# A two layer trunk kernel: the first weights issued from ScalarE's queue, and the half empty weight units stored densely

## The chip, the cores and the metric

The kernel runs on one core of one Trainium2 chip. The metric is device time in microseconds (us) of one execution. A core has five engines that run side by side and meet through semaphores: TensorE (PE, matrix products; its weight loads are listed as PEld), VectorE (DVE), ScalarE (ACT), GpSimd (POOL) and SyncE (SP), which here does nothing but issue DMAs. DMAs move data between HBM and the on-chip memory SBUF; SP, ACT and POOL can each issue them, every one into a queue of its own.

## What is computed

The reference is a trunk of two layers on 512 tokens of width 1024, in float32. Each layer is a mixer and a feed-forward block, each followed by a residual and a layer norm:

```
h = x
for layer in (0, 1):
    mix = even_mixer(h) if layer == 0 else odd_mixer(h)
    h = layer_norm(ALPHA * h + mix)
    h = layer_norm(ALPHA * h + conv_ffn(h))

even_mixer: x @ w_in -> conv + silu -> gated delta rule (6 heads), with beta = sigmoid(b), g from a
            x @ w_in -> dilated attention (3 groups, 4 heads);  concat @ w_out
odd_mixer:  x @ w_in -> differential attention (4 heads)
            x @ w_in -> gated linear attention (4 heads), its gate from g_d;  concat @ w_out
```

What matters here is the first product. The even mixer's narrow columns `b_a` and `a_a` (6 and 6) and the key columns of head 0 are needed for all 512 tokens before anything else can begin. The odd mixer has such a narrow piece too: the 16 columns `g_d`.

## The kernel before

All weights lie in one tensor `wts` of 128 x 1024 float32 units (512 KB each). A unit is eight blocks of 128 x 128, one for each 128 rows of the contraction (`k` = 0 to 7). The units 0 (`U_AB`: the columns of `b_a` and `a_a`) and `U_GG` (the columns `g_d`) are called NARROW: of each block only 64 columns hold anything, the other 64 are zeros.

Float32 products are made of float32r parts. A tile `x` of tokens becomes `xh` (a rounding CAST on ACT, line 252) and `xl = x - xh` (DVE, line 253). A weight unit becomes `wh` (ACT, line 493) and `wl` (DVE, line 494). A full unit costs three matmuls for each `k` (`mm3`, lines 481 to 483). A narrow unit keeps its high and low parts side by side in one tile, 64 columns each, and costs two (`narrow`, lines 501, 502 and 504).

`setup` (from line 205) starts everything. The tuple `START` gives the order in which the eight token tiles `("x", a, a + 1)` (256 KB each, 2 KB to a partition) and pieces of the first two units `(i, a, e)` (blocks `a` to `e` of unit `i`) are loaded. A first loop over `START` issues the loads, all of them on SP's queue (lines 223 and 226): 14 DMAs. Eight matmuls on a constant tile follow (`warm`, line 234). A second loop over `START` emits the CAST and the subtraction of each piece in the same order. Then `ask` asks for the units 2 and 3, whose loads (line 340) stand behind those of `START` on SP's queue, and the tables `par` and `con` follow (lines 261 and 262). Raw units pass through three buffers `wr`; units 0 and 1 hold two of them, so unit 2 takes the third and unit 3 waits until the last piece of unit 0 has been split.

`even` then emits the first products, `narrow` of step `k` ahead of `mm3` of step `k - 1`:

```
for k in range(KD + 1):
    if k < KD:
        self.narrow(pa, wa, k, self.xh[:, k, :], self.xl[:, k, :])
    if k:
        self.mm3(pb, wb, k - 1, ...)
```

After them come the tiles of the next units (`tile_of`, matmuls at line 366), with chains of other work in between, which a planner places by costs of its own. The chain `gates` takes the narrow product `pa` first; it begins with the load of an activation table (line 408). Instructions emitted through the planner all show line 159.

The order of instructions on an engine is the framework's: it lets an instruction forward when its simulated inputs are there earlier. `tc.keep_in_program_order` pins an instruction behind the one that was emitted before it on the same engine.

`U_GG` is loaded much later, by `unit` (line 474) inside the layer norm that ends layer 0, ahead of the odd mixer's first products in `lead`.

Of the kernel before, what the change touches and what calls it, by code (L numbers as in the profile page):

```python
# [9 lines left out]
F32 = mybir.dt.float32  # L10
# [7 lines left out]
P = 128  # L18
# [3 lines left out]
KD = D // P  # L22
# [36 lines left out]
for _n, _w in (("ident", 128), ("maskT", 128), ("nm1", 32), ("i32", 32), ("lm", 4 * 32), ("scan", 512),  # L59
# [30 lines left out]
EVEN_SEQ = "h0 h1 h2 h3 h4 h5 q00 v0 q01 v1 q02 v2 q10 q11 q12 z0 z1 z2 z3 z4 z5"  # L90
ODD_SEQ = "0D12G3abcd"

START = (("x", 0, 1), (0, 0, 2), ("x", 1, 2), (1, 0, 2), (0, 2, 5), ("x", 2, 3), ("x", 3, 4), (1, 2, 5), ("x", 4, 5),
         (0, 5, 8), ("x", 5, 6), ("x", 6, 7), (1, 5, 8), ("x", 7, 8))
WARM = 8
LEAD = 3
AHEAD = 2
# [97 lines left out]
class Trunk:  # L195
# [14 lines left out]
    def setup(self):  # L210
# [7 lines left out]
        self.xh = keep.tile([P, KD, S], F32R, name="xh")  # L218
        self.xl = keep.tile([P, KD, S], F32R, name="xl")
        first = [(u, self.wtiles()) for u in (U_AB, U_AB + 1)]  # L220
        for what, a, e in START:
            if what == "x":
                nc.sync.dma_start(self.h[:, a, :], self.xt[:, a, :])
            else:
                u, w = first[what]
                nc.sync.dma_start(w[0][:, a * P : e * P], self.wts[u][:, a * P : e * P])
        self.par = keep.tile([P, _NP], F32, name="par")
        self.con = keep.tile([P, _NCC], F32, name="con")
        self.ones = keep.tile([P, P], F32, name="ones")
        nc.gpsimd.memset(self.ones, 1.0 / P)  # L230

        warm = self.sps("warm")
        for _ in range(WARM):
# [233 lines left out]
    def unit(self, u, pool=None):  # L467
        nc = self.nc
        if u in self.asked:
            self.until(lambda: u in self.pre)  # L470
        if u in self.pre:
            return self.pre.pop(u)
        raw, wh, wl = self.wtiles(pool)
        nc.sync.dma_start(raw, self.wts[u])
        self.split(u, raw, wh, wl, nc.scalar, nc.vector)
        return wh, wl

# [7 lines left out]
    def split(self, u, raw, wh, wl, A, V, w=slice(0, KD * P)):  # L485

        if u in NARROW:
            raw, lo = (x[:, w].rearrange("p (k n) -> p k n", n=P) for x in (raw, wh))
            hi = lo[:, :, 0:64]
            raw, lo = raw[:, :, 0:64], lo[:, :, 64:P]  # L490
        else:
            raw, hi, lo = raw[:, w], wh[:, w], wl[:, w]
        A.copy(out=hi, in_=raw)  # L493
        V.tensor_tensor(out=lo, in0=raw, in1=hi.bitcast(F32), op=ALU.subtract)  # L494
# [1395 lines left out]
def _units(a):  # L1890
    def cols(w, off, n=P):

        x = w[:, off : off + n]
        if n < P:
            x = np.concatenate([x, np.zeros((w.shape[0], P - n), np.float32)], 1)
        return x

    def tile8(x, order=range(8)):
        b = x.reshape(8, P, P)
        return np.concatenate([b[k] for k in order], 1)  # L1900

    we, wo = a["w_in_even"][0], a["w_in_odd"][0]
    us = []

    def by_token(x):

        b, n = x.reshape(KD, P, x.shape[1]), 1024 // x.shape[1]
        for k in range(0, KD, n):
            us.append(np.concatenate(list(b[k : k + n]), 1))

    gq, gk, gv, gz, gb, ga = 0, 768, 1536, 2304, 3072, 3078
    ab = np.zeros((D, P), np.float32)
    ab[:, 0:6] = we[:, gb : gb + 6]
    ab[:, 32:38] = we[:, ga : ga + 6]
    us.append(tile8(ab))
    for h in range(6):
        for off in (gk, gq, gv):
            us.append(tile8(cols(we, off + h * P)))
    s0 = 3084
    for pair in range(2):  # L1920
        for g in range(3):
            for kind in range(2):
                us.append(tile8(cols(we, s0 + kind * 768 + g * 256 + pair * P)))
    for g in range(3):
        x = s0 + 2 * 768 + g * 256
        if g == 0:
            by_token(we[:, x : x + 256])
        else:
            for pair in range(2):
                us.append(tile8(cols(we, x + pair * P)))  # L1930
    for h in range(6):
        us.append(tile8(cols(we, gz + h * P)))
    for ft in range(8):
        us.append(tile8(cols(a["w_out_even"][0], ft * P), EVEN_ORDER))

    def ffn(l):
        up, dn = a["ffn_w_up"][l], a["ffn_w_down"][l]
        for f in range(NF):
            us.append(tile8(cols(up, f * P)))
            us.append(tile8(cols(up, DFF + f * P)))  # L1940
        b = dn.reshape(NF, P, 8, P).transpose(2, 0, 1, 3).reshape(22, 8, P, P)
        for u in range(22):
            us.append(np.concatenate(list(b[u]), 1))

    ffn(0)
    us.append(tile8(cols(wo, 3072, 16)))
    for pr in range(2):
        us.append(tile8(cols(wo, 1536 + pr * P)))
        us.append(tile8(cols(wo, 1792 + pr * P)))
    by_token(wo[:, 2048:2560])  # L1950
    by_token(wo[:, 1024:1536])
    for h in range(4):
        for off in (0, 512):
            us.append(tile8(cols(wo, off + h * P)))
    for h in range(4):
        us.append(tile8(cols(wo, 2560 + h * P)))
    for ft in range(8):
        us.append(tile8(cols(a["w_out_odd"][0], ft * P), ODD_ORDER))
    ffn(1)
    return np.ascontiguousarray(np.stack(us))  # L1960
# [31 lines left out]
```

## Time and profile before

| what | us |
|---|---|
| median of 3 runs | 1426.18 |
| lowest and highest of them | 1426.1, 1427.62 |
| the profiled execution's own time | 1425.01 |
| its span, first to last instruction | 1423.2 |
| TensorE busy in it | 1401.0 (98%) |

The profiled execution has 1.81 us outside its span, and it is 1.17 us below the median of the runs. A product of 512 columns takes PE 0.23 us from one start to the next, so the first products, 40 of them, are worth some 9.3 us of work.

In the rows below, a row of the order in time reads: start, duration, engine, line, operation, tiles, shape, how many, and in brackets how long the engine had been idle and what ended that. SPq and ACTq are DMA issues, whose duration is that of the issue and not of the transfer.

### The profile page before, as it was taken

How to read it: one execution, taken by the hardware profiler on the slowest of the kernel's cores; microseconds unless marked ns; L12 is line 12 of the kernel's file. 1: busy time of each engine (PE TensorE's matmuls, PEld its weight loads, DVE VectorE, ACT ScalarE, POOL GpSimd, SP SyncE). 2: the span in 40 equal slices, each digit the busy share in tenths (PEclk: the TensorE clock that was granted, in tenths of full speed). 3: DMA queues.
4: the chain of work that ended last, by engine and by line, in shares of the span. 5: the costliest groups of instructions: out<-in, count | busy, mean ns of one | idle time of the engine just before them, and what ended most of it. 6: DMA issues, size and time to landing. Idle time of an engine off the chain costs nothing.

```text
span 1423.2 us, 22725 instructions
## 1 busy us (share of the span) xinstructions
PE 1401.0 (98%) x9050; PEld 1146.4 (81%) x9050; DVE 840.7 (59%) x1636; ACT 673.9 (47%) x1285; POOL 177.6 (12%) x237
## 2 busy tenths in 40 slices
PE   8999999999999999999999999999999999999997
PEld 6878887777798888888888877878898888888886
DVE  6875755543696555555243797777776555553354
ACT  6644433744856444434131856557574444442233
POOL 2103012011023111111010310000131111110010
PEclk9999999999999999999999999999999999999998
DMA  7444112112232232232223313211313223223221
GB/s 248 151 130 125 61 50 72 55 61 65 90 119 90 89 97 95 90 99 94 96 97 104 92 55 105 74 46 60 119 38 120 95 90 100 93 89 104 89 74 59
DMA packets 41601, 130.94 MB, mean 92 GB/s; under 512 B 4653, under 2 KB 9629, under 8 KB 41496
## 3 DMA queue, kind: packets, MB, share of 16 engines
q1 hardware_dynamic: 36448, 120.36, 26.2%
q10 hardware_dynamic: 3464, 4.14, 1.1%
q0 software_dynamic: 1584, 5.00, 1.1%
q8 instruction: 71, 1.16, 0.3%
q14 instruction: 34, 0.28, 0.1%
HBM read 127.29 MB, written 5.29 MB: 93 GB/s over the span
## 4 chain that ended last, share of the span: by engine, by line
PE 84%; DVE 6%; ACT 5%; DMA 2%; issue 2%; POOL 1%; SPq 0%; ACTq 0%; DVEq 0%; POOLq 0%
PE pd L481 18%; PE pd L482 18%; PE pd L483 18%; PE pd L366 17%; PE pd L392 3%; PE pc L159 1%; PE po L159 1%; PE sps L159 1%; PE pz L159 1%; PE py L159 1%; DMA wr<-wts 1%; PE dsc L159 1%; PE pa L159 1%; PE dpo L159 1%; DVE s L553 1%
## 5 line engine op out<-in xcount | busy, mean ns | idle before, releaser
L494 DVE TENSOR_TENSOR wl<-wr,wh 128x1024 fp32r<-128x1024 f32 (+1 forms) x153 | 188.0, 1230 | 314.1 <-ACT wh L493 310.5
L481 PE MATMUL pd<-xh,wh 128*128 128x512 f32 (+1 forms) x968 | 356.4, 369 | 1.3 <-ACT wh L493 0.8
L482 PE MATMUL pd<-xl,wh 128*128 128x512 f32 (+1 forms) x968 | 357.0, 369 | 0.3 <-DVE xl L678 0.2
L483 PE MATMUL pd<-xh,wl 128*128 128x512 f32 (+1 forms) x968 | 356.3, 368 | 0.0
L493 ACT CAST wh<-wr 128x1024 fp32r<-128x1024 f32 (+2 forms) x157 | 160.0, 1025 | 208.5 <-PE pd L482 184.4
L482 PEld LDWEIGHTS pd<-xl,wh 128*128 128x128 f32 x968 | 181.6, 188 | 35.4 <-DVE xl L678 0.9
L481 PEld LDWEIGHTS pd<-xh,wh 128*128 128x128 f32 x968 | 181.3, 188 | 35.7 <-ACT wh L493 1.2
L483 PEld LDWEIGHTS pd<-xh,wl 128*128 128x128 f32 x968 | 181.6, 188 | 34.6 <-issue 0.8
L366 PE MATMUL pd<-xh,wh 128*128 128x512 f32 x424 | 173.0, 408 | 0.0
L366 PE MATMUL pd<-xl,wh 128*128 128x512 f32 x424 | 171.4, 404 | 0.0
L481 PE MATMUL pd<-ah,wh 128*128 128x512 f32 (+1 forms) x396 | 145.1, 366 | 0.0
L483 PE MATMUL pd<-ah,wl 128*128 128x512 f32 (+1 forms) x396 | 144.7, 365 | 0.0
L482 PE MATMUL pd<-al,wh 128*128 128x512 f32 (+1 forms) x396 | 144.7, 365 | 0.0
L715 DVE SCALAR_TENSOR_TENSOR y<-pd,par,y 128x510 f32<-128x510 f32 (+1 forms) x176 | 130.6, 747 | 2.8
L366 PE MATMUL pd<-xh,wl 128*128 128x512 f32 x424 | 118.8, 404 | 0.0
L724 POOL TENSOR_TENSOR al<-y,ah 128x512 fp32r<-128x512 f32 x44 | 59.1, 1343 | 419.8 <-ACT ah L723 419.8
L159 DVE TENSOR_TENSOR wl<-wr,wh 128x1024 fp32r<-128x1024 f32 x63 | 77.1, 1226 | 37.6 <-PE pd L366 14.7
L159 ACT CAST wh<-wr 128x1024 fp32r<-128x1024 f32 x63 | 65.8, 1047 | 61.4 <-PE pd L366 44.4
L366 PEld LDWEIGHTS pd<-xl,wh 128*128 128x128 f32 x424 | 79.8, 188 | 17.3 <-issue 1.9
L366 PEld LDWEIGHTS pd<-xh,wh 128*128 128x128 f32 x424 | 79.7, 188 | 16.9 <-issue 0.3
L366 PEld LDWEIGHTS pd<-xh,wl 128*128 128x128 f32 x424 | 76.4, 188 | 15.7 <-issue 0.7
L482 PEld LDWEIGHTS pd<-al,wh 128*128 128x128 f32 x396 | 74.7, 189 | 12.2
(386 smaller groups left out, 1866.9 us busy)
## 6 DMA issues: line engine op xcount, KB each, us to landing
wr<-wts SPq DMA_DIRECT2D x214, 512.0 KB, 3.4
h<-xt SPq DMA_DIRECT2D x16, 256.0 KB, 3.7
rep<-tab POOLq DMA_DIRECT2D x1, 3072.0 KB, 17.2
h<-gd POOLq DMA_DIRECT2D x6, 256.0 KB, 6.3
qe<-ge ACTq DMA_DIRECT2D x5, 256.0 KB, 6.1
bd<-rep ACTq DMA_DIRECT2D x1, 1024.0 KB
out<-h SPq DMA_DIRECT2D x2, 512.0 KB, 3.0
wr<-wts SPq DMA_DIRECT2D x4, 192.0 KB, 5.7
```

The lines of the kernel that those rows point to most:

```text
L159: r = fn(*a, **k)
L366: self.nc.tensor.matmul(ps, lhsT=w[part][:, k * P : (k + 1) * P], rhs=x[:, k, :], start=(i == 0), stop=(i == 23))
L392: self.nc.tensor.matmul(pss[b][:, a : a + n], lhsT=chunk(x[:, k, :], c), rhs=ws, start=(k == 0 and a == 0 and not part and x is self.xh), ...
L481: nc.tensor.matmul(ps, lhsT=wh, rhs=ah, start=first, stop=False)
L482: nc.tensor.matmul(ps, lhsT=wh, rhs=al, start=False, stop=False)
L483: nc.tensor.matmul(ps, lhsT=wl, rhs=ah, start=False, stop=last)
L493: A.copy(out=hi, in_=raw)
L494: V.tensor_tensor(out=lo, in0=raw, in1=hi.bitcast(F32), op=ALU.subtract)
L553: V.tensor_tensor(out=s2[:, a:e], in0=(self.q0 if ft == 1 else s2)[:, a:e], in1=q[:, : e - a], op=ALU.add)
L715: V.scalar_tensor_tensor(out=y[:, sft:], in0=ps[:, : S - sft], scalar=w(2 - sft), in1=y[:, sft:], op0=ALU.mult, op1=ALU.add)
L724: G.tensor_tensor(out=al[:, f, :], in0=y, in1=ah[:, f, :].bitcast(F32), op=ALU.subtract)
```

## The change

The loads of the first two units move from SP's queue to ACT's; the token tiles stay on SP's. On ACT they are pinned, in `START`'s order, behind a copy of one column (`idle`), which needs the constant tile `ones`; that tile's memset is emitted earlier for it. `START` itself is rewritten: unit 0 is loaded in two pieces and not three, so that there are 13 DMAs, eight on SP and five on ACT. The two narrow units are stored densely: eight blocks of 64 columns, then 512 columns of zeros. Their loads (in `setup` and in `unit`) take the first half only, 256 KB, and `split` reads the raw tile densely. The split parts, the products and everything after them stay.

```diff
-START = (("x", 0, 1), (0, 0, 2), ("x", 1, 2), (1, 0, 2), (0, 2, 5), ("x", 2, 3), ("x", 3, 4), (1, 2, 5), ("x", 4, 5),
-         (0, 5, 8), ("x", 5, 6), ("x", 6, 7), (1, 5, 8), ("x", 7, 8))
+START = (("x", 0, 1), (0, 0, 4), ("x", 1, 2), (1, 0, 2), ("x", 2, 3), (1, 2, 5), ("x", 3, 4), (0, 4, 8), ("x", 4, 5),
+         ("x", 5, 6), (1, 5, 8), ("x", 6, 7), ("x", 7, 8))
...
         first = [(u, self.wtiles()) for u in (U_AB, U_AB + 1)]
+
+        self.ones = keep.tile([P, P], F32, name="ones")
+        nc.gpsimd.memset(self.ones, 1.0 / P)
+        idle = keep.tile([P, 1], F32, name="idle")
+        tc.keep_in_program_order(nc.scalar.copy(out=idle, in_=self.ones[:, 0:1]))
         for what, a, e in START:
             if what == "x":
                 nc.sync.dma_start(self.h[:, a, :], self.xt[:, a, :])
             else:
+
                 u, w = first[what]
-                nc.sync.dma_start(w[0][:, a * P : e * P], self.wts[u][:, a * P : e * P])
+                n = 64 if u in NARROW else P
+                tc.keep_in_program_order(nc.scalar.dma_start(w[0][:, a * n : e * n], self.wts[u][:, a * n : e * n]))
         self.par = keep.tile([P, _NP], F32, name="par")
         self.con = keep.tile([P, _NCC], F32, name="con")
-        self.ones = keep.tile([P, P], F32, name="ones")
-        nc.gpsimd.memset(self.ones, 1.0 / P)
...
         raw, wh, wl = self.wtiles(pool)
-        nc.sync.dma_start(raw, self.wts[u])
+        n = KD * (64 if u in NARROW else P)
+        nc.sync.dma_start(raw[:, :n], self.wts[u][:, :n])
         self.split(u, raw, wh, wl, nc.scalar, nc.vector)
...
         if u in NARROW:
-            raw, lo = (x[:, w].rearrange("p (k n) -> p k n", n=P) for x in (raw, wh))
-            hi = lo[:, :, 0:64]
-            raw, lo = raw[:, :, 0:64], lo[:, :, 64:P]
+            lo = wh[:, w].rearrange("p (k n) -> p k n", n=P)
+            raw = raw[:, w.start // 2 : w.stop // 2].rearrange("p (k n) -> p k n", n=64)
+            hi, lo = lo[:, :, 0:64], lo[:, :, 64:P]
...
+    def narrow(x):
+
+        b = x.reshape(8, P, P)[:, :, :64]
+        return np.concatenate(list(b) + [np.zeros((P, 512), np.float32)], 1)
+
...
-    us.append(tile8(ab))
+    us.append(narrow(ab))
...
-    us.append(tile8(cols(wo, 3072, 16)))
+    us.append(narrow(cols(wo, 3072, 16)))
```

## Rows read from the trace of the kernel before

**Rows 1.** Busy time by stretch: length, engines (instructions), TensorE's clock, DMA share, GB/s.

```profile
0.00:5.20 5.20, 3.79 (x17) 3.50 (x17) 1.68 (x4) 2.10 (x3) 4.42 (x16) 1.00 0.53 151
5.20:18.10 12.90, 10.94 (x41) 6.98 (x41) 7.46 (x14) 9.28 (x17) 0.00 (x0) 1.00 0.99 335
18.10:1423.20 1405.10, 1386.29 (x8995) 1135.88 (x8993) 831.57 (x1619) 662.52 (x1267) 173.17 (x221) 1.00 0.28 90
```

**Rows 2.** The order in time on PE, 1 to 18.4 us.

```profile
1.01 3.79 PE L234 MATMUL warm<-ones 128*128 128x128 f32 x16 [1.01 <-POOL ones L230]
5.20 0.58 PE L501 MATMUL pd<-xh,wh 128*128 128x512 f32 x1 [0.40 <-DVE wh L494]
5.61 0.39 PE L502 MATMUL pd<-xl,wh 128*64 128x512 f32 x1
...
8.03 0.50 PE L481 MATMUL pd<-xh,wh 128*128 128x512 f32 x1 [0.84 <-ACT wh L493]
...
10.31 0.44 PE L502 MATMUL pd<-xl,wh 128*64 128x512 f32 x1 [0.23 <-DVE xl L253]
...
12.91 0.45 PE L502 MATMUL pd<-xl,wh 128*64 128x512 f32 x1
...
16.46 0.39 PE L502 MATMUL pd<-xl,wh 128*64 128x512 f32 x1
...
18.10 0.39 PE L366 MATMUL pd<-xh,wh 128*128 128x512 f32 x1
```

**Rows 3.** The order in time on ACT, 0 to 35 us.

```profile
0.75 1.28 ACT L252 ACT_TABLE_LOAD   x1 [0.75 <-PEq L1984]
3.60 0.62 ACT L252 CAST xh<-h 128x512 fp32r<-128x512 f32 x1 [1.56 <-DMA h<-xt]
...
7.57 0.40 ACT L493 CAST wh<-wr 128x256 fp32r<-128x256 f32 x1 [1.61 <-DMA wr<-wts]
...
8.92 0.62 ACT L252 CAST xh<-h 128x512 fp32r<-128x512 f32 x1 [0.42 <-DMA h<-xt]
9.44 0.19 ACT L159 CAST rp<-rb 33x4 fp32r<-33x4 f32 x1
...
14.52 0.62 ACT L252 CAST xh<-h 128x512 fp32r<-128x512 f32 x1 [0.16 <-DMA h<-xt]
15.16 1.28 ACT L408 ACT_TABLE_LOAD   x1
16.45 1.05 ACT L159 CAST wh<-wr 128x1024 fp32r<-128x1024 f32 x1
...
34.07 1.05 ACT L159 CAST wh<-wr 128x1024 fp32r<-128x1024 f32 x1 [0.94 <-PE pd L366]
34.08 0.84 ACTq L1128 DMA_DIRECT2D qe<-ge  x2
```

**Rows 4.** Busy time by stretch again, while the first loads run.

```profile
4.00:7.00 3.00, 2.36 (x8) 1.14 (x7) 1.59 (x3) 1.03 (x3) 0.96 (x2) 1.00 0.66 177
7.00:14.00 7.00, 5.28 (x20) 3.17 (x19) 4.37 (x10) 4.77 (x11) 0.00 (x0) 1.00 1.08 364
```

**Rows 5.** SP: its second issue, then what its queue waited for (us, times, longest).

```profile
1.19 0.42 SPq L226 DMA_DIRECT2D wr<-wts  x1
...
SPq L223 <- DMA wr<-wts: 1.0, 1, 1.0
```

**Rows 6.** The order in time on DVE: the subtraction of a piece of 128x256.

```profile
8.01 0.43 DVE L494 TENSOR_TENSOR wl<-wr,wh 128x256 fp32r<-128x256 f32 x1 [1.32 <-ACT wh L493]
```

**Rows 7.** Groups of 780 to 808 us, the odd mixer's narrow products: busy, mean ns, idle.

```profile
L501 PE MATMUL pd<-xh,wh 128*128 128x256 f32 x14 | 3.9, 278 | 0.0
```

**Rows 8.** Waits of PE over the whole span, the longest (us, times, longest).

```profile
PE pvt L159 <- ACT vf L159: 1.7, 1, 1.7
```

**Rows 9.** The trace's end: PE's last matmuls, then a stretch as in rows 1.

```profile
1412.42 0.59 PE L617 MATMUL sd<-sq,onesL 128*128 128x256 f32 x2
...
1415.00:1416.00 1.00, 0.00 (x0) 0.00 (x0) 1.00 (x5) 0.72 (x2) 0.50 (x1) 0.54 0.00 0
```

## The prediction

> **What bounds the kernel now.** I read busy time by stretch first. From 18.10 us to the end TensorE is busy 1386.29 of 1405.10 us [rows 1]: it sets the time, its work does not change here, and only 18.8 us in all are not matmul, the tail after its last product among them. So the change can act only by letting TensorE start that run earlier, and every microsecond gained before 18.10 is kept unless something else is late next.
>
> Before 18.10 the order in time on PE shows what is to be won. The seven starts from 16.46 to 18.10 give 0.234 us for one matmul; 40 of them are 9.4 us, and they take from 5.20 to 18.10, 12.9 us [rows 2]. So 3.5 us are lost. The reader is to see where: the subtraction of the first weights ends the wait at 5.20, the first piece of unit 1 that at 8.03 (0.84 us), and the low part of token tile 2 that at 10.31. From there to 12.91 stand ten steps, 2.34 us of work in 2.60, so tile 4 costs only 0.26 more; from 12.91 on there is no gap: 22 steps, 5.15 us, to 18.10. All of these are waits for DMAs behind ACT and DVE: ACT's CASTs of tile 0, of the piece at 7.57, of tile 2 and of tile 7 each begin when their transfer lands [rows 3].
>
> Busy time by stretch shows how the transfers run. From 7 to 14 us they move 364 GB/s with the DMA engines full (1.08); from 4 to 7 us it is 177 GB/s at a share of 0.66 [rows 4]. SP's queue at times waits for an earlier landing before it issues again (1.0 us once) [rows 5].
>
> **The change, part by part.**
>
> *Fewer bytes.* START falls from 3072 to 2816 KB (8 x 256 and 512 + 512, then 256 + 512). At 364 KB per us the whole group lands 0.7 us earlier, tile 7 with it, at some 13.8 and not 14.5 [rows 3, 4]. But tile 7 is not what TensorE waits for: after 12.91 it has no gap [rows 2]. What counts is how much is moved before tile 2, and then before tile 4. In the old order 1216 KB are moved up to the end of tile 2 (three tiles, pieces of 128, 128 and 192 KB) and 1920 up to that of tile 4. Now the weights come on a queue of their own, so the order is no longer given. If they come just as START lists them, it is 1024 and 1856 KB: 0.53 and 0.18 us earlier. If the two queues take turns packet by packet from the start, tile 2 ends with three pieces of weights as before (1216 KB, 0), and tile 4 with all five (2048 KB, 0.35 us later). The trace of before has no stretch with both queues full, so I keep both ends and take 0: the old order is almost in the middle.
>
> By the Trainium skill (DMA: Bandwidth & Descriptors, Queues, rings and completion order) each DMA engine goes round between the queues that have work, a packet at a time; by it the second end holds, and the sum would be 0.35 us later through tile 4. No run here shows it yet.
>
> *Two queues in the slow stretch.* From 4 to 7 us the engines moved 3 x (364 - 177) = 561 KB less than at the later rate, 1.54 us of transfer [rows 4]. This is before tile 2 lands at 8.92, so all that is gained there moves tile 2, tile 4 and TensorE. If one queue alone was what left the engines idle, a second one fills the stretch: 1.54 us. If it was the transfers themselves (SP had issued enough of them, and waited for landings [rows 5]), it gives nothing. I take half, 0.8 us.
>
> *Later first weights.* ACT's queue begins with the table load, 0.75 to 2.03, and the copy (nearest row 0.19, the CAST of 33x4) [rows 3]. The first piece is then issued at about 2.2 instead of 1.19 [rows 5], and it is twice as many blocks: CAST and subtraction of 128x256 take 0.40 and 0.43 [rows 3, 6], of which what the smaller piece took falls away. So the first matmul comes between 6.2 and 7.0 instead of 5.20; if ACT issues beside the table load, as it issues at 34.08 beside a CAST that began at 34.07 [rows 3], at about 5.2. I take 6.4. It costs nothing: four matmuls stand before the wait at 8.03, and 6.4 + 4 x 0.234 is 7.3. The cover is that wait; without it the 1.2 us would be paid.
>
> *Five issues on ACT.* One takes 0.42 us, since two take 0.84 [rows 3]. From 2.2 they would last to 4.3, and what is queued behind them is the CAST of tile 0, at 3.60 before; the low part, the split of unit 0 and the first matmul wait for that. At most 0.7 us, inside the same cover. A last piece that must wait for a landing, as SP's did for 1.0 us [rows 5], would hold all CASTs behind it; ACT is busy 9.28 of 12.90 us there [rows 1], so 1.0 us more fits too, if the order of the CASTs lets it.
>
> *SP's queue.* It issues six DMAs fewer ahead of tile 7, and units 2 and 3 and the tables come sooner. What is next to be late is unit 2 on ACT: CAST of tile 7, table load, CAST of unit 2, from 14.52 to 17.50, where TensorE arrives at 18.10 [rows 2, 3]. This has 0.6 us to spare and moves with tile 7, which comes 0.7 us earlier by the bytes alone; so it holds a gain of up to 1.3, and more if the slow stretch fills.
>
> *The other narrow unit.* Its load is halved, 256 KB. The odd mixer's narrow matmuls had no idle time before them [rows 7], so this is worth 0; the cover is that the unit is loaded and split while the layer norm's last products still run. Dense reads by `split` have the same number of elements: 0.
>
> The sum: 0.8 (slow stretch) + 0 (order) + 0 (the rest, covered). From the profiled execution's 1425.0 this gives 1424.2. That execution is 1.2 below the median, so from 1426.2 the prediction is 1425.4. Its own bounds are 0 to 1.5 of gain, less where tile 4 is late: 1424.7 to 1426.1. About 0.2% (2.85 us) is what a measurement of this kernel can tell from no change; all of this lies within it.
>
> **The rivals.**
>
> *The same transfers at the same pace.* The engines are full from 7 us on [rows 4], and the slow stretch belongs to them and not to the queue. Then tile 2 lands when it did: 1426.2. For it: SP's waits for landings. Against it: a share of 0.66 with work issued.
> By the Trainium skill (DMA: Bandwidth & Descriptors, Issuing engines are not separate DMA queues) DMAs issued from several engines run on the same DMA engines, and only the issuing time is saved; by it this rival holds. The share of 1.08 with one queue agrees.
>
> *The slow stretch vanishes and the list's order holds.* 1.54 + 0.53 = 2.1 us: 1424.1. TensorE's own limit allows it: 6.4 + 9.4 = 15.8, a gain of 2.3; with a first matmul at 5.2 it would be 3.5. Against it: both ends at once.
>
> *Slower: the first weights come so late that TensorE's clock falls.* After the last matmul (1412.42 + 0.59) the granted clock stays at full until about 1415.1, some 2.1 us later (0.54 over 1415 to 1416), and goes to half, 1.2 GHz [rows 9]. The warm-up ends at 4.80 [rows 2], so a first matmul after 6.9 decides it; the upper end above is 7.0. A matmul then takes 0.47. How long it stays low no row shows; the nearest is the warm-up's 3.8 us of work. From 7.0 with 3.8 us at half speed (8 matmuls) and 32 at 0.234 the end is 18.3, 0.2 later; with twice that time it is 20.2, 2.1 later. In the middle 1.2 later: 1427.4. Against it: the stretch 5.20 to 18.10 has gaps and stays at 1.00 [rows 1].
>
> *Another order further on.* The framework orders by simulated times: the CAST of `rp` stands on ACT at 9.44, between token tiles, though it belongs to a chain planned for later [rows 3]. Other landing times may exchange neighbours on ACT or DVE in the work that follows. Its price is that of a single new wait or of one that goes away; PE's longest is 1.7 us [rows 8]. 1424.5 or 1427.9.
>
> **How the numbers follow.** Forecast 0.46, the same pace 0.20, the full gain 0.15, the clock 0.09, another order 0.10, half to each side. The likeliest gives 1425.4. The range reaches over the full gain (1424.1, with the 0.8 below it that an earlier first matmul or an order of luck would add) and over the clock and the worse order (1427.4 and 1427.9): 1423.3 to 1427.8 leaves out some 0.15. Faster by over 0.2% means below 1423.3: a third of the full gain and half of the better order, and a little for what I don't see, 0.12. Slower means above 1429.0: the upper part of the clock's price and a worse order, 0.06. The rest, 0.82, is no change.
>
> **What would show it.** In the changed kernel's profile: more than 177 GB/s from 4 to 7 us (the gain), or not (the same pace); the first L366 start at about 17.3; the first matmul between 5.2 and 7.0 with the clock at 1.00 behind it; the wait for tile 2 still the last large one; unit 2's CAST ended before TensorE asks; no idle time at the odd mixer's L501; the run after L366's start as long as before, 1405.1 us. The prediction is wrong if that run changes by over 1 us (another order), or if tile 4 or a held CAST comes to stand behind 12.9 us.

## The result: 1411.6 us, faster by 1.1%

The changed kernel's median is 1411.55 us over 4 runs (1409.85 to 1412.89), that of the kernel before beside it 1426.9: a ratio of 0.9892, 95% interval 0.988 to 0.9905. The profiled execution's span is 1411.1 us, 12.1 shorter. In the profile after, line numbers are 5 or 6 higher: 366 is 371, 481 to 483 are 487 to 489, 501 and 502 are 507 and 508.

Busy time by stretch of the changed kernel, columns as in [rows 1, 4] and with the same borders; the first stretch is left out:

```profile
...
5.20:18.10 12.90, 10.95 (x41) 8.36 (x42) 8.40 (x15) 9.64 (x18) 0.00 (x0) 1.00 0.99 352
18.10:1411.10 1393.00, 1370.95 (x8994) 1139.32 (x8993) 830.11 (x1618) 662.42 (x1266) 175.40 (x221) 1.00 0.28 90
4.00:7.00 3.00, 0.79 (x4) 0.49 (x3) 0.93 (x2) 1.58 (x4) 0.94 (x2) 1.00 0.99 334
7.00:14.00 7.00, 6.84 (x23) 5.10 (x24) 5.77 (x12) 5.14 (x11) 0.00 (x0) 1.00 1.07 365
```

The slow stretch of the transfers is gone: 334 GB/s from 4 to 7 us, where it was 177. But the time did not come from there. The stretch behind 18.10 lasts 1393.0 us and not 1405.1, and TensorE is busy 15.3 us less in it, of which 3.2 return as idle time, with the same number of matmuls to within one (x8994, x8995). The same work takes it less time.

The order in time on PE, as in [rows 2], shows that the start won next to nothing:

```profile
1.01 3.78 PE L239 MATMUL warm<-ones 128*128 128x128 f32 x16 [1.01 <-POOL ones L223]
7.16 0.79 PE L507 MATMUL pd<-xh,wh 128*128 128x512 f32 x1 [2.37 <-DVE wh L500]
...
10.31 0.44 PE L507 MATMUL pd<-xh,wh 128*128 128x512 f32 x1
...
17.91 0.39 PE L371 MATMUL pd<-xh,wh 128*128 128x512 f32 x1
```

The first matmul comes at 7.16, two us later than before, and the first seven then take 3.15 us to 10.31, 0.45 each, about twice the usual step. This is the lower clock, 1.2 GHz, by the steps alone: in the second profile below, steps of 0.43 us stand from 8.80 to 13.93, where the granted clock reads 0.50, while the clock column of this stretch reads 1.00. From 10.31 on there is no gap. The first L371 starts at 17.91, 0.19 us earlier than its counterpart.

The order in time on ACT, as in [rows 3], says why the first matmul was late:

```profile
0.99 1.35 ACTq L233 DMA_DIRECT2D wr<-wts  x3
...
4.01 1.36 ACTq L233 DMA_DIRECT2D wr<-wts  x2
5.42 0.62 ACT L257 CAST xh<-h 128x512 fp32r<-128x512 f32 x1 [3.19 <-DMA h<-xt]
...
17.30 1.05 ACT L159 CAST wh<-wr 128x1024 fp32r<-128x1024 f32 x1 [1.14 <-DMA wr<-wts]
```

ACT issued three loads beside its table load, which runs from 0.75 to 2.03, then the fourth only at 4.01. The CAST of tile 0 stands behind the fifth, at 5.42. The view puts its wait down to the tile's landing; an experiment below puts 1.5 us of it down to the issues.

Where the 12 us went can be read by the starts of landmarks. Before: the layer norm's first product after layer 0's output projection, the first down product, the layer norm behind the second output projection, and the first down product of layer 1.

```profile
415.18 0.66 PE L615 MATMUL mean<-s,onesL 128*128 128x256 f32 x2
669.31 0.39 PE L481 MATMUL pd<-ah,wh 128*128 128x512 f32 x1
1034.66 0.70 PE L615 MATMUL mean<-s,onesL 128*128 128x256 f32 x2
1288.96 0.39 PE L481 MATMUL pd<-ah,wh 128*128 128x512 f32 x1
```

And after:

```profile
415.52 0.59 PE L621 MATMUL mean<-s,onesL 128*128 128x256 f32 x2
663.46 0.39 PE L487 MATMUL pd<-ah,wh 128*128 128x512 f32 x1
1028.69 0.70 PE L621 MATMUL mean<-s,onesL 128*128 128x256 f32 x2 [0.69 <-DVE s L563]
1276.74 0.39 PE L487 MATMUL pd<-ah,wh 128*128 128x512 f32 x1
```

Up to 415 us nothing is won. From the first landmark to the second, the up projection of layer 0, it is 254.13 us before and 247.94 after; from the third to the fourth, that of layer 1, it is 254.30 and 248.05. These two stretches hold 12.4 us, the whole gain. In between, from the second landmark to the third, it is 365.35 and 365.23. The diff touches no line that the up projections run.

Busy time of PE alone within the up projection and within the down projection (length, PE busy and instructions, clock, DMA share, GB/s), before:

```profile
450.00:650.00 200.00, 200.00 (x859) 1.00 0.30 98
680.00:770.00 90.00, 90.00 (x398) 1.00 0.31 100
```

and after:

```profile
450.00:650.00 200.00, 200.00 (x884) 1.00 0.31 100
680.00:770.00 90.00, 90.00 (x403) 1.00 0.31 97
```

TensorE has no idle time in either, at full clock, and yet it does 884 matmuls of 512 columns in 200 us where it did 859: a step of 0.226 us and not 0.233. In the down projection it was already fast (90 / 398 is 0.226). An up projection has 41 units of 24 such matmuls, 984; times 0.0066 us this is 6.5 us, about the 6.2 seen.

### The profile page after: what moved, and what is told of

It is laid out like the page before. It is cut to its first block, busy times and chain, and to the rows that moved or that the text cites. A ratio compares the mean times of both kernels' runs of the same rounds, so it can differ in the third digit from the quotient of the medians.

```text
span 1411.1 us, 22721 instructions
## 1 busy us (share of the span) xinstructions
PE 1385.7 (98%) x9050; PEld 1151.2 (82%) x9050; DVE 839.3 (59%) x1635; ACT 673.5 (48%) x1285; POOL 179.8 (13%) x237
## 4 chain that ended last, share of the span: by engine, by line
PE 83%; DVE 6%; ACT 5%; DMA 3%; issue 2%; POOL 1%; ACTq 0%; DVEq 0%; POOLq 0%
PE pd L487 18%; PE pd L488 18%; PE pd L489 17%; PE pd L371 16%; PE pd L397 3%; DMA wr<-wts 2%; PE pc L159 1%; PE po L159 1%; PE sps L159 1%; PE pz L159 1%; PE py L159 1%; PE pa L159 1%; PE dsc L159 1%; DVE wl L159 1%; PE dpo L159 1%
## 5 line engine op out<-in xcount | busy, mean ns | idle before, releaser
L499 ACT CAST wh<-wr 128x1024 fp32r<-128x1024 f32 (+1 forms) x156 | 159.8, 1030 | 196.7 <-PE pd L488 171.4
L371 PE MATMUL pd<-xh,wh 128*128 128x512 f32 x424 | 172.7, 407 | 0.0
L371 PE MATMUL pd<-xl,wh 128*128 128x512 f32 x424 | 170.9, 403 | 0.0
L371 PE MATMUL pd<-xh,wl 128*128 128x512 f32 x424 | 117.8, 402 | 0.0
L371 PEld LDWEIGHTS pd<-xl,wh 128*128 128x128 f32 x424 | 80.5, 190 | 16.2 <-issue 1.9
L371 PEld LDWEIGHTS pd<-xh,wh 128*128 128x128 f32 x424 | 80.4, 190 | 15.7 <-issue 0.3
L371 PEld LDWEIGHTS pd<-xh,wl 128*128 128x128 f32 x424 | 76.4, 188 | 14.6 <-issue 0.7
L487 PEld LDWEIGHTS pd<-ah,wh 128*128 128x128 f32 x396 | 74.7, 189 | 12.2
```

The lines of the kernel that those rows point to most:

```text
L371: self.nc.tensor.matmul(ps, lhsT=w[part][:, k * P : (k + 1) * P], rhs=x[:, k, :], start=(i == 0), stop=(i == 23))
L487: nc.tensor.matmul(ps, lhsT=wh, rhs=ah, start=first, stop=False)
```

## What else the diff changes: where the weights lie

`idle` is a new tile in the pool `keep`, ahead of the weight buffers in a partition. Its one float takes 32 bytes, as `cst` with its three does, and all tiles allotted behind it move by 32 bytes. From the beginning of `xh` to that of the first `wh` there lie, before: `xh` and `xl` (32768 bytes), `ones`, `onesL` and two more of 128 floats (2048), `par` (496 floats, 1984), `con` (1088 floats, 4352), `cst` (32) and three raw buffers (12288): 53472 bytes, which is 209 x 256 less 32. With `idle` it is 53504, exactly 209 x 256. The four `wh` and four `wl` take 4096 each, and the down projection's `ah` follows them directly: it lies like the weights in both kernels, and its step was 0.226 in both.

So the theory, called place: a matmul's step depends on whether the moving tile and the stationary one begin at the same byte of a partition modulo some power of two (128 in the expectations). The rival, called loads: the new queue, the dense units and the order that follows from them bring the 12 us. The experiments part them; in the expectations "alike" means the same place modulo 128.

## The experiments: the tile without the loads, the loads without the tile

**The kernel before with 32 bytes more.** Nothing of the change but its side effect:

```diff
         nc.gpsimd.memset(self.ones, 1.0 / P)
+        pad = keep.tile([P, 1], F32, name="pad")
+        nc.gpsimd.memset(pad, 0.0)
```

> The kernel before with one more tile of 32 bytes behind the constant `ones` and nothing else, so that the weight buffers lie 32 bytes further on, as they do in the changed kernel; all loads as before. Place theory (the matmul step depends on where the weight tiles lie against the token tiles): the step of the products on xh and xl falls from 0.234 to 0.227 us, the first L366 still starts at 18.1, and the time falls by 12 to 15 us, to 1411 to 1415. Loads theory (the second queue and the dense units made the gain): the step stays at 0.234 and the time at 1426 to 1428.

Measured: 1412.9 us (1411.81 to 1413.4), ratio 0.9904 [0.9889, 0.9919]. PE in the up projection and the transfers from 4 to 7 us:

```profile
450.00:650.00 200.00, 200.00 (x884) 1.00 0.31 100
...
4.00:7.00 3.00, 2.21 (x8) 1.05 (x7) 1.59 (x3) 1.19 (x3) 0.94 (x2) 1.00 0.77 198
```

The first product of the third unit (L368 here, L366 in the kernel before) was expected at 18.1 and comes at 20.36, with the granted clock at 0.61 from 7 to 14 us:

```profile
20.36 0.39 PE L368 MATMUL pd<-xh,wh 128*128 128x512 f32 x1
```

So an unused tile and its memset bring what the whole change brought, with the loads nearly as slow as before and a start that is 2.3 us later. The loads theory falls. That it is not the memset shows further down: the same tile and memset ahead of all tiles bring nothing.

**The changed kernel without its 32 bytes.** `idle` becomes the fourth column of `cst`, so that the weights lie as before:

```diff
-        idle = keep.tile([P, 1], F32, name="idle")
+        self.cst = keep.tile([P, 4], F32, name="cst")
+        idle = self.cst[:, 3:4]
...
-        self.cst = keep.tile([P, 3], F32, name="cst")
```

> The changed kernel with `idle` put into a column of a tile that exists anyway, so that the weight buffers lie where they lay before; all its loads and its dense units stay. Place theory: the step is 0.234 again and the time is that of the kernel before or up to 3 us more, since the new wait at pg stays: 1425 to 1430. Loads theory: 1410 to 1413.

Measured: 1425.97 us (1425.09 to 1426.81), ratio 0.9994 [0.9985, 1.0004]. Its rows:

```profile
450.00:650.00 200.00, 200.00 (x859) 1.00 0.30 98
...
4.00:7.00 3.00, 0.79 (x4) 0.49 (x3) 0.82 (x2) 1.47 (x4) 0.94 (x2) 1.00 1.05 369
```

The transfers run at 369 GB/s and the step is back at 0.233: all that the change says it does is worth 0.6 us between the medians (1426.53 for the kernel before beside it), by the interval between 2.1 won and 0.6 lost.

**The five loads back on SP, and the changed kernel again.** In the changed kernel the loads of the first weights go to SP's queue, in the new order; beside it the changed kernel itself:

```diff
-                tc.keep_in_program_order(nc.scalar.dma_start(w[0][:, a * n : e * n], self.wts[u][:, a * n : e * n]))
+                nc.sync.dma_start(w[0][:, a * n : e * n], self.wts[u][:, a * n : e * n])
```

> The changed kernel with one thing undone: the five loads of the first weights are issued on SP's queue again, in the new order of START; the dense units and the extra tile stay, so the weights keep the tokens' place. If the second queue is worth nothing in the end, as the run with the weights at their old place had it: 1411.5, within 2 us of the changed kernel that runs beside it. If the second queue gives what the half term of the prediction said: 0.8 us slower than the changed kernel, and up to 1.5. The stretch from 4 to 7 us should then fall back from 334 to some 180 GB/s.

> The changed kernel itself once more, on the chip of the three runs beside it: 1411.6, a ratio of 0.989 to the kernel before. It is there to be compared with the loads back on SP's queue.

Measured on one chip: 1411.59 us (1410.14 to 1412.69), ratio 0.989 [0.9874, 0.9907], with the loads on SP; 1410.71 (1409.63 to 1412.02), ratio 0.9887 [0.9872, 0.9902], for the changed kernel. The 0.9 us between the medians is within the spread of either, so the 0.8 us of the prediction's half term is neither shown nor ruled out. With the loads on SP the stretch and the first matmul are:

```profile
4.00:7.00 3.00, 1.82 (x7) 0.92 (x6) 1.35 (x3) 1.22 (x3) 0.80 (x2) 1.00 0.69 199
...
5.41 0.49 PE L507 MATMUL pd<-xh,wh 128*128 128x512 f32 x1 [0.62 <-DVE wh L500]
```

and in the second profile of the changed kernel:

```profile
4.00:7.00 3.00, 0.44 (x4) 0.25 (x3) 0.00 (x0) 0.52 (x1) 0.80 (x2) 1.00 0.99 344
7.00:14.00 7.00, 5.79 (x14) 4.11 (x15) 6.42 (x12) 5.90 (x14) 0.00 (x0) 0.53 1.08 350
...
8.21 0.79 PE L507 MATMUL pd<-xh,wh 128*128 128x512 f32 x1 [3.77 <-DVE wh L500]
...
20.24 0.39 PE L371 MATMUL pd<-xh,wh 128*128 128x512 f32 x1
```

So the queue alone makes the 334 to 344 GB/s, and the later first matmul too (5.41 against 7.16 and 8.21). The granted clock is below 1.00 from 7 to 14 us with either queue: 0.53 in the second profile, 0.76 with the loads on SP, where steps of 0.43 us run from 9.19 to 12.17. The end shows none of this.

**Two pieces back on SP.** The last piece of each unit, the two that ACT issued from 4.01 on, goes to SP's queue:

```diff
+                if e > 5 or (what, a) == (0, 4):
+                    nc.sync.dma_start(w[0][:, a * n : e * n], self.wts[u][:, a * n : e * n])
+                    continue
```

> The changed kernel with the last piece of each of the first two units issued from SP's queue, at its place in START, so that only three loads stand on ACT ahead of the CASTs and none of them has to wait for a landing. The hold on ACT goes: the CAST of tile 0 begins at some 4.1 us and not 5.42, the first matmul at 5.3 to 6.0 and not 7.16, the first matmul of the third unit at 15.3 to 16.8 and not 17.9. If TensorE's start is what sets the time of the even mixer: 1409 to 1411 (changed kernel 1411.6). If the even mixer is paced by its chains on the other engines, as its unchanged end at 401.8 us with the shorter matmul step suggests: first lnp product still at 401 to 402, 1411 to 1413.

Measured: 1412.92 us (1412.1 to 1415.04), ratio 0.9908 [0.9893, 0.9922], so no better. Its rows on ACT, then on PE:

```profile
3.93 0.62 ACT L260 CAST xh<-h 128x512 fp32r<-128x512 f32 x1 [1.70 <-DMA h<-xt]
...
5.56 0.71 ACT L502 CAST wh<-wr 128x256 fp32r<-128x256 f32 x2
...
6.78 0.80 PE L510 MATMUL pd<-xh,wh 128*128 128x512 f32 x1 [1.98 <-DVE wh L503]
...
17.64 0.39 PE L374 MATMUL pd<-xh,wh 128*128 128x512 f32 x1
...
L588 PE MATMUL lnp<-hi,onesK x4: 394/394/394, 401.8 to 1340.3; 128*128 128x512 f32 x4
```

The CAST of tile 0 no longer stands behind issues and begins at 3.93 instead of 5.42: 1.49 us of hold, as said above. But now the second tile's CAST (5.04) has been let forward, ahead of the first weights' at 5.56, and the first matmul gains only 0.38 us, the first L374 0.27; both come later than expected. And even that is lost: the last row is the list of one tile's matmuls (first and last start), and the first, the end of the even mixer's last tiles, starts at 401.8, as it does before (its list says 401.8 to 1352.9) and after (401.8 to 1340.7).

In the second profile of the changed kernel, whose first L371 came 2.3 us later, it is 401.0. In the changed kernel, what is won or lost in the first 18 us is not what arrives at 402.

## The experiments: which places count

Five kernels move tiles only, by unused tiles as above: 32 bytes behind `idle` in the changed kernel; 32 ahead of all tiles in the kernel before; both 32 ahead of all and 32 behind `ones`; 96 bytes behind `ones`; and 32 between the buffers of `wh` and those of `wl`, in the kernel before and then in the changed kernel:

```diff
-                wp.tile([P, 1024], F32R, name=self.nm("wh"), tag="wh", bufs=n),
-                wp.tile([P, 1024], F32R, name=self.nm("wl"), tag="wl", bufs=n))
+        wh = wp.tile([P, 1024], F32R, name=self.nm("wh"), tag="wh", bufs=n)
+        if not self.padded:
+            self.padded = self.wp.tile([P, 1], F32, name="pad", tag="pad", bufs=1)
+            self.nc.gpsimd.memset(self.padded, 0.0)
+        return raw, wh, wp.tile([P, 1024], F32R, name=self.nm("wl"), tag="wl", bufs=n)
```

> The changed kernel with one more tile of 32 bytes, so that the weight buffers lie 64 bytes further on than before, 32 off a multiple of 64 again, while xh and xl stay on a multiple of 64. Place theory in the form that the places within 64 bytes count: step 0.234, 1425 to 1430. Place theory in the form that only the old place was bad: step 0.227, 1410 to 1413. Loads theory: 1410 to 1413.

> The kernel before with a tile of 32 bytes ahead of everything: xh and xl move to 32 off a multiple of 64, the weights to a multiple of 64, their distance stays as before. If what counts is that weights and tokens lie alike within 64 bytes: step 0.234 on xh and xl, 1425 to 1429, no gain. If what counts is that the weights begin on a multiple of 64: step 0.227, 1411 to 1415. Loads theory: 1426 to 1428.

> The kernel before with 32 bytes ahead of everything and 32 more ahead of the weights: tokens and weights both lie 32 off a multiple of 64. If weights and tokens must lie alike within 64 bytes: step 0.227 on xh and xl, 1411 to 1415. If both must begin on a multiple of 64: step 0.234, 1425 to 1429.

> The kernel before with a tile of 96 bytes behind `ones`: the weights lie on a multiple of 64 that is 64 off a multiple of 128, the tokens on a multiple of 128. If places within 64 bytes count: step 0.227, 1411 to 1415. If places within 128 bytes count: step 0.234, 1425 to 1429.

> The kernel before with 32 bytes between the buffers wh and wl: wh lies unlike the tokens, wl alike. Read in the up projections, where each k has xh by wh, xl by wh, xh by wl. If a matmul is slow by its own weights' place: the steps of the first two 0.234, that of the third 0.227. If it is slow by the place of the weights that are loaded while it runs, those of the next matmul: the second 0.227, the first and the third 0.234. The down projections' tokens come to lie unlike wh, so the whole time is near that of before by either: 1424 to 1430.

> The changed kernel with 32 bytes between the buffers of wh and those of wl: xh, xl and wh begin at 0 modulo 128, wl at 32, and ah and al at 32 too. It is the mirror of the run with wl alone alike. The theory that the high weights decide (two of three matmuls of a product use them): the up projections stay at 0.2267 us a step or lose at most a third of the gain, the down projections become slow, near 1416 us. The theory that all that meet in a product must be alike: up and down projections both at 0.233, as with wl alone alike, near 1430 us.

The distances from the tokens' first byte to that of `wh` and of `wl`, modulo 256, follow from the sum above and the bytes added. The count is that of PE's matmuls from 450 to 650 us, as in the rows shown:

| kernel | `wh` | `wl` | matmuls | median us | ratio |
|---|---|---|---|---|---|
| before | -32 | -32 | 859 | 1426.9 | 1 |
| after | 0 | 0 | 884 | 1411.55 | 0.9892 |
| before, 32 more | 0 | 0 | 884 | 1412.9 | 0.9904 [0.9889, 0.9919] |
| after, 32 less | -32 | -32 | 859 | 1425.97 | 0.9994 [0.9985, 1.0004] |
| after, 32 more | 32 | 32 | 858 | 1426.74 | 1.0005 [0.9995, 1.0015] |
| before, 32 ahead of all | -32 | -32 | 859 | 1427.02 | 1.0004 [0.9994, 1.0013] |
| before, 32 ahead of all, 32 more | 0 | 0 | 884 | 1412.14 | 0.9897 [0.9881, 0.9914] |
| before, 96 more | 64 | 64 | 858 | 1426.23 | 0.9998 [0.9989, 1.0007] |
| before, `wl` alone moved | -32 | 0 | 859 | 1430.73 | one run |
| after, `wl` alone moved | 0 | 32 | 859 | 1430.34 | one run |

Only the three with both distances at 0 are fast. With 32 bytes ahead of all, the weights begin on a multiple of 128 and the tokens don't: slow. With 32 more behind that, neither begins on a multiple of 64: fast. So it is the distance that counts, not where a tile begins. A distance of 64 is slow too, so it has to be taken modulo more than 64.

The last two are the surprise. With only one of the two weight parts alike, a product of three matmuls is as slow as with none, and the down projections become slow too, since `ah` and `al` move along with `wl`. With `wl` alone moved in the kernel before:

```profile
680.00:770.00 90.00, 90.00 (x388) 1.00 0.31 100
```

388 matmuls where before had 398. If a matmul's own weights or those of the next decided, one in three, or two, would be fast. Of what was expected only the last form fits: all that meet in a product must lie alike.

## The experiments: matmuls by themselves

Two kernels leave out the whole trunk and do nothing but matmuls, 96 to a group (192 with 256 columns), each group twice; the core of the second (in the first, `wb` is one number):

```python
for i in range(count):
    o = (wb[i % len(wb)] if isinstance(wb, tuple) else wb) // 4 + (0 if still else i % 8 * P)
    b = (xb[i % len(xb)] if isinstance(xb, tuple) else xb) // 4
    nc.tensor.matmul(ps[:, 0:cols], lhsT=w[:, o : o + P], rhs=x[:, b : b + cols], start=i == 0, stop=i == count - 1)
```

> This kernel leaves out the whole trunk. Its only work is matmuls of float32r, 128x128 by 128x512, all from one moving tile x and one stationary tile w, with no transfer and no other engine at work beside them. Each group is 96 matmuls (192 with 256 columns), and the byte at which the moving columns and the weights begin, modulo 128, is set by hand: aa 0 and 0, ab 0 and 32, ac 0 and 64, ad 0 and 96, ah 0 and 16, ba 32 and 0, bb 32 and 32, bd 32 and 96; mixed takes moving columns at 0 and 32 in turn with weights at 0; still keeps one weight block for all its matmuls (0 and 32); halfa and halfb are aa and ab with 256 columns. The theory that the places alone set the step, inside TensorE: aa and bb at 0.2267 us a step (21.8 us busy a group), ab, ac, ad, ba and bd at 0.233 (22.4), mixed between. If the weights' load beside the moving columns is what collides, still is as slow as ab, since each matmul loads its weights again; if it is only the moving columns against PSUM or the sequencer, no group differs. The rival, that the places matter only when ACT, DVE or DMAs use the memory beside TensorE: all groups of 512 columns take the same, 21.8 us.

> Again only matmuls of float32r from one moving tile x and one stationary tile w; the whole trunk is left out. Start bytes modulo 128 of moving columns and weights by group, 96 matmuls each, names in brackets taken in turn: wa 0 and (0, 32); wb 0 and (0, 0, 32), the pattern of the run with wh alone alike; now (0, 32) with (0, 32), so that each matmul is alike with its own weights and unlike with those of the next; next (0, 32) with (32, 0), the reverse; aa 0 and 0; far 0 and 128; ab 0 and 32; near 0 and 8; swap 0 and (32, 64); halfd, halfa and halfe with 256 columns at 0 and 64, 0 and 0, 32 and 32. Theory that a matmul's own weights decide: now 0.2267 us a step, next 0.2333, wa 0.230, wb 0.2289. Theory that the weights loaded meanwhile decide: now 0.2333, next 0.2267, wa 0.230, wb 0.2289. Theory that the weights have to lie at one place throughout, whatever matmul they belong to: wa and wb 0.2333, and now and next no better than 0.230. If places count modulo 128, far is 0.2267 like aa; if modulo 256, it is 0.2333. If blocks of 16 or 32 bytes count and not the byte, near is 0.2267. The run with wh alone alike speaks for the third, with a mean of 0.2333 a step in its up projections.

The groups of the first, by the name of their result (busy us, mean ns of one, idle before). Each group of 512 columns has 192 matmuls, so 1.3 us between two groups are 0.0068 us a step:

```profile
L1818 PE MATMUL ac<-x,w 128*128 128x512 f32 x192 | 45.1, 396 | 0.0
...
L1818 PE MATMUL ab<-x,w 128*128 128x512 f32 x192 | 45.1, 395 | 0.0
L1818 PE MATMUL still<-x,w 128*128 128x512 f32 x192 | 45.1, 395 | 0.0
...
L1818 PE MATMUL mixed<-x,w 128*128 128x512 f32 x192 | 44.5, 392 | 0.0
L1818 PE MATMUL bb<-x,w 128*128 128x512 f32 x192 | 43.8, 389 | 0.0
```

`aa`, the first group of all, began with steps of twice the length and is not compared; `bb` stands for alike. The effect is TensorE's own: with no transfer and no other engine at work, alike (`bb`) is 43.8 us, 32 or 64 bytes apart 45.1, with one weight block for all matmuls as well, and moving tiles that alternate lie between. 1.3 of 43.8 is 3.0%, the 0.233 against 0.226 of the trunk. The rival, contention with other engines, falls.

The groups of the second:

```profile
L1818 PE MATMUL halfa<-x,w 128*128 128x256 f32 x384 | 46.4, 283 | 0.0
...
L1818 PE MATMUL wb<-x,w 128*128 128x512 f32 x192 | 45.1, 395 | 0.0
...
L1818 PE MATMUL far<-x,w 128*128 128x512 f32 x192 | 44.9, 395 | 0.0
L1818 PE MATMUL now<-x,w 128*128 128x512 f32 x192 | 44.8, 394 | 0.0
L1818 PE MATMUL swap<-x,w 128*128 128x512 f32 x192 | 44.7, 393 | 0.0
L1818 PE MATMUL near<-x,w 128*128 128x512 f32 x192 | 44.6, 393 | 0.0
L1818 PE MATMUL next<-x,w 128*128 128x512 f32 x192 | 44.5, 392 | 0.0
...
L1818 PE MATMUL aa<-x,w 128*128 128x512 f32 x192 | 43.9, 389 | 0.0
L1818 PE MATMUL halfd<-x,w 128*128 128x256 f32 x384 | 43.9, 276 | 0.0
```

`far` is slow: 128 bytes apart is not alike. In the trunk 209 x 256 is, so the distance counts modulo 256, and not 128 as I had supposed. `wb`, two matmuls alike and the third not, is as slow as none alike (45.1), as in the trunk, where two thirds of 1.3 would have been won by each matmul's own weights. `now` and `next` are both between: neither the weights in use nor those loaded meanwhile decide alone. But `swap`, whose weights lie at 32 and 64 in turn and never alike, is between too (44.7), so being partly alike is not what shortens them. In the other direction, the second group of `wa`, weights at 0 and 32 in turn, takes 22.71 us for its 96, more than `ab` (22.56; `aa` 21.94); its first group began with steps of twice the length. What a sequence of changing places costs is measured here and not explained. `near` shows that even 8 bytes cost more than half of it. With 256 columns it is the other way round: alike (`halfa`) is slowest, 64 bytes apart (`halfd`) 2.5 us faster in 384.

**A version with its halves at 64 bytes.** Three feature tiles of each output projection and the last one of each down projection are made in halves of 256 columns. In the changed kernel their own weight pools get room for an offset:

```diff
+HALVED = [u + i for u in (U_OE, U_OO) for i in (5, 6, 7)] + [U_D0 + 21, U_D1 + 21]
...
+        n0, o = (1088 if pool else 1024), (16 if pool and u in HALVED else 0)
...
-                wp.tile([P, 1024], F32R, name=self.nm("wh"), tag="wh", bufs=n),
+                wp.tile([P, n0], F32R, name=self.nm("wh"), tag="wh", bufs=n)[:, o : o + 1024],
```

and `wl` likewise.

> The changed kernel, with one more change of places: the weights of the output projections' last three feature tiles and of the last down unit, whose products are made in halves of 256 columns, begin 64 bytes behind the tokens' place modulo 256; all others stay alike. With matmuls alone a step of 256 columns took 0.1200 us alike and 0.1133 us at 64 bytes. If this holds in the trunk, the 384 matmuls concerned (two layers of 144 and 48) win 2.5 us: about 1409, and the 256 column products between 402 and 415 us start 0.113 us apart. If the place of 512 column products alone counts in the trunk, where ACT, DVE and DMAs are at work too: 1411.6 and no change there.

Measured: 1410.54 us (1410.4 to 1410.75), ratio 0.9893 [0.9876, 0.9909]: not to be told from the changed kernel. Two starts in the last tiles of the output projection, ten steps apart:

```profile
405.72 0.28 PE L489 MATMUL pd<-xh,wh 128*128 128x256 f32 x1
...
406.90 0.28 PE L490 MATMUL pd<-xl,wh 128*128 128x256 f32 x1
```

This is 0.118 us a step; in the changed kernel ten steps there take 1.20 us (nine from 405.80 to 406.88: 0.120). Of the 0.0065 us won alone (2.5 us in 384), 0.002 arrive, 0.8 us in the 384 of the trunk. Why so little, no run shows. In the kernel before, at a distance of -32, ten steps there took 1.17 us (405.73 to 406.90), so the changed kernel gives some of its gain back in these halves. No version here beats the changed kernel by what can be measured.

## Why the prediction was wrong

The time, 1411.55, is outside the range, 1423.3 to 1427.8, and no rival of the prediction had it.

- **The step that failed** is the first one: from 18.10 us on TensorE "sets the time, its work does not change here", and so only an earlier start could gain. TensorE does set the time in the up projections, and its instructions do not change. But the step from one to the next does: 0.233 to 0.226 us in both up projections, 12.4 us. In the part by part, the copy was costed as an instruction on ACT (0.19 us) and not as a tile that moves all tiles behind it. The prediction's own sign of being wrong, that the run behind 18.10 changes by over 1 us, came (1405.1 to 1393.0), but not for the reason it gave, another order. The rows already held a hint: steps of 0.234 us in the prologue, and the down projection of the same form at 0.226 in the same trace, which I did not compare.
- **The slow stretch.** The half term was mis-sized: from 4 to 7 us 334 GB/s arrive, so 3 x (365 - 334) = 93 KB are missing and not 561, and 1.3 us of the 1.54 are won in transfer, not 0.8. The queue does it: 199 GB/s with the same loads on SP. The engines, at a share of 0.66 with one queue, stand at 0.99, so the rival of the same pace is wrong about the transfers. By the Trainium skill (DMA: Bandwidth & Descriptors, Issuing engines are not separate DMA queues) a second issuing engine saves only the time of issuing, which is usually small. Here that time may be all of it, and it was not small: by 3.04 us SP alone had issued five DMAs (960 KB), the two queues eight (1728 KB). Whether anything else in a queue slowed it, no run parts.
- **The first weights on ACT.** ACT did issue beside its table load, at 0.99, but the last two issues came at 4.01, held the CAST of tile 0 for 1.5 us (0.7 had been said, and 1.0 more if a landing had to be waited for), and the first matmul came at 7.16, outside the 5.2 to 7.0. What the fourth issue waited for, the trace does not show. The cover then failed in the way of the slower rival, at half speed: seven matmuls took 3.15 us and not 1.6. Its price was 0.2 to 2.1 us. In the first profile it does not show, since only seven matmuls were slow and nothing was waited for after 7.16: the first L371 starts at 17.91, against 18.10. In the second, fourteen took 6.07 us, and the first L371 starts at 20.24, 2.1 later. Its condition, a first matmul after 6.9, is not borne out: the granted clock fell to half as well behind first matmuls at 5.36 (32 bytes more) and 5.41 (loads on SP). That the kernel before held 1.00 to 18.10 is what one profile of it shows.
- **"Every microsecond gained before 18.10 is kept"** holds nearly with the old step, and not with the short one. From one profile each, the start of the third unit's first product and of the first `lnp` product at the end of the even mixer:

| kernels, in order | third unit | `lnp` |
|---|---|---|
| long step: before; after, 32 less; after, 32 more; before, 96 more; before, 32 ahead of all | 18.10, 18.22, 19.00, 19.50, 20.96 | 401.8, 401.8, 402.6, 403.4, 404.0 |
| short step: two pieces on SP; after; loads on SP; halves at 64; before, 32 ahead of all, 32 more; after again; before, 32 more | 17.64, 17.91, 18.43, 18.59, 19.81, 20.24, 20.36 | 401.8, 401.8, 401.1, 399.6, 401.7, 401.0, 402.1 |

  With the long step the time between is 383.0 to 383.9 us, so a late start arrives at the end. With the short step it is 380.8 to 384.2, and the two earliest starts take longest. The even mixer holds 936 products of 512 columns behind the third unit's start; at 0.0066 us each they should win an estimated 6.2 us, and of that at most 3 arrive. What absorbs the rest is not settled. From 18.20 to 402 TensorE is idle 8.1 us in the changed kernel and 6.2 before. New waits stand in between, such as this one of PE, from the waits over the whole span, at 28 us; from 31 to 34 us the clock, in the stretch below it, is at half:

```profile
PE pg L159 <- ACT wh L159: 1.5, 1, 1.5
```
```profile
31.00:34.00 3.00, 3.00 (x9) 2.33 (x8) 2.68 (x5) 1.49 (x3) 2.66 (x5) 0.50 0.35 89
```

- **Right**: the bytes, the reordered list and the other narrow unit are worth nothing that shows. Unit 2's CAST ends at 16.07, ahead of 17.91, and at the odd mixer's narrow products of 774 to 802 us nothing waits, as in [rows 7]:

```profile
L507 PE MATMUL pd<-xh,wh 128*128 128x256 f32 x14 | 3.9, 279 | 0.0
```

  Without the 32 bytes the change gives 1425.97, and the prediction was 1425.4. That they are near is not the sum come true: in that profile the first L371 starts at 18.22, where some 17.3 was foreseen.
- **Open**: what inside TensorE makes the step depend on the distance, and on that of its neighbours in the sequence; and why the even mixer's products gain so little. And between the landmarks of 669 and 1035 us before, where the two kernels agree to 0.12 us, parts may have moved against each other.

## What to carry to other kernels

Where one engine is busy without a gap, compare the step of the same instruction between stages of one trace before taking its time as given; a difference of 3% (0.233 against 0.226 us) was worth more than all waits of the prologue. In a kernel bound by 512 column float32r products, lay moving tiles and both weight parts at one place modulo 256 bytes (in the up projections that was worth 12.4 us, in the even mixer next to nothing), and look at it again after any edit that adds a tile, however small. When a change pays more than its own steps can, make its side effects alone: an unused tile of 32 bytes gave 1412.9 of 1426.5 us.

## What the runs showed of the hardware

- A 512 column matmul of float32r in a row of its like takes 0.2267 us a step when moving and stationary tile begin at the same byte modulo 256, and 0.233 us at distances of -32, 16, 32, 64 and 96 bytes (45.1 to 45.3 against 43.8 us in 192).
- With 256 columns the order is reversed: 46.4 us in 384 alike, 43.9 at 64 bytes.
- The place has to be one for the whole sequence: with two matmuls of three alike, 192 took 45.1 us, as with none alike.
- The same first loads ran at 199 GB/s from 4 to 7 us from one queue, and at 334 and 344 GB/s from two.
- An issue that comes late holds the work behind it on ACT: with five loads the fourth was issued 1.67 us after the third had ended, and the first CAST began at 5.42; with three it began at 3.93.
- A step of 512 columns is 0.43 us where the granted clock reads 0.50 and 0.227 to 0.234 where it reads 1.00. In the first 16 us the clock differs between kernels with the same loads: 1.00 from 7 to 14 us in the kernel before, 0.61 in the one with 32 bytes more.
